# The second pair of feed-forward chunks in seven products, begun on half of the tokens, and three sums of x on GpSimd

## The chip, the cores and the metric

One core of a Trainium2 chip runs the whole kernel. The metric is device time in microseconds (us), the median of several runs. The engines are named as in the profile: PE is TensorE's matmul, PEld its weight load, DVE is VectorE, ACT ScalarE, POOL GpSimd, SP SyncE, which here only starts transfers.

## The reference

A decoder trunk of two layers over 512 tokens of width 1024, in float32. Each layer is a feed-forward (FFN), a mixer (attention and retention) and a second FFN, each followed by a layer norm of the scaled input plus the branch:

```python
def swiglu_ffn(x, w_gu, w_down):
    a, u = jnp.split(x @ w_gu, 2, axis=-1)
    return (jax.nn.silu(a) * u) @ w_down
...
    for l in range(DEPTH):
        x = layer_norm(DEEPNORM_ALPHA * x + 0.5 * swiglu_ffn(x, ffn1_w_gu[l], ffn1_w_down[l]), ln1_g[l], ln1_b[l])
        x = layer_norm(DEEPNORM_ALPHA * x + hybrid_mixer(x, w_in[l], w_out[l], ...), ln2_g[l], ln2_b[l])
        x = layer_norm(DEEPNORM_ALPHA * x + 0.5 * swiglu_ffn(x, ffn2_w_gu[l], ffn2_w_down[l]), ln3_g[l], ln3_b[l])
```

The hidden width of an FFN is 2816: 22 chunks of 128, taken as 11 pairs. There are four FFNs, called A, B, C and D here in the order of time. A begins the program, B follows the first mixer, C follows B directly, and D follows the second mixer.

## The kernel before

**Three matmuls for one.** Every operand is split into a high part (`uh`, `xh`, rounded to the fast matmul type by ACT) and the rest (`ul`, `xl`, a subtraction on DVE); `split` (L173, L174) does both. `mm3` (L188 to L190) multiplies high by high, high by low and low by high into one PSUM bank (`ps`).

**Units.** A weight unit is a split block of 1024 x 128. `Weights` emits the splits of the next units in a given order, up to six units held at once, and loads of 1 MB (`raw`, two buffers, on SP's queue) ahead of them; `done` releases units and so lets the next ones be split. A raw buffer is free for the next load when its last split has read it.

**x and the norms.** x is kept transposed, as `xh` and `xl`, in eight blocks of 128 features by 512 tokens. Each norm (`norm`, DVE, with one small power on GpSimd, L521) finishes 128 tokens of `Y`; `y_to_xT` then transposes them on PE (L488), 8 transposes for 128 tokens, and splits them in two pieces of four blocks each. The transposes run after a number of `step`s of the matmul loops (a task that is `spawn`ed with a delay) or where `finish` forces them out; `pend` holds the four tasks of one norm.

**The gate and up phase (`ffn`).** Before, the first pair of chunks (`fp == 0`) is plain: `glu` makes a and u of one chunk for half of the tokens, 48 matmuls of 256 columns, then silu on ACT and a multiplication on DVE (`gate`, L630 and L631). The second pair (`fp == 1`) is plain too: chunk 2 in halves of the tokens, its a already between the parts of the first pair (`more`), chunk 3 over all 512 columns. From the third pair on (`SEVEN`), `glu7` takes seven block products where the plain form takes eight: x and the weights are cut in 2 x 2 blocks, and sums of blocks are multiplied. A pair then is 14 products of 12 matmuls of 256 columns. Before the first of these pairs, `lead` (L460) issues four matmuls whose result is overwritten.

**Sums of x.** `sums_of_x` makes the sums once per FFN: four additions `xh + xl` (L556), 1024 columns each, into unused chunks of the hidden tile `hT`, then four differences (L560), each split into `Th`, `Tl`. All are on DVE but the high parts. `B[0][0]` and `B[1][0]` are of the first half of the tokens, `B[0][1]` and `B[1][1]` of the second.

**Sums of the weights.** `seven_items` lists a pair's seven units: the first a and u units (`first`), the sums of a (`s12`, `s34`), the last blocks of both (`last`), the sums of u. One `s12` or `s34` pair makes four DVE operations of 512 columns into `S` (L321, L322, L325, L326).

**Order.** A scheduler orders each engine's instructions by the program's order, taking a later one where an earlier is not ready by its own times; each engine then runs its list strictly in order. `mm3`, and until `pin` is cleared the splits too, are held behind what was traced before them on their engine.

Of the kernel before, what the change touches and what calls it, by code (L numbers as in the profile page):

```python
# [15 lines left out]
SEQ = 512  # L16
D = 1024
DFF = 2816
P = 128
# [14 lines left out]
SEVEN = (2, 3, 4, 5, 6, 7, 8, 9, 10)  # L34
# [65 lines left out]
class Trunk:  # L100
# [247 lines left out]
    def ffn_items(self, gu, down, key):  # L348
        items = []
        for fp in range(NFP):  # L350
            a = self.cols_item(gu, fp * 256, (key, "a", fp))
            u = self.cols_item(gu, DFF + fp * 256, (key, "u", fp))
            if fp == 0:
                items += [a[0], u[0], a[1], u[1]]
            else:
                items += self.seven_items(a, u) if fp in SEVEN else a + u
# [179 lines left out]
    def ffn(self, g_, b, out=None):  # L536
        nc, tc, W = self.nc, self.tc, self.W
        with ExitStack() as ctx:
# [8 lines left out]

            def sums_of_x():

                x = hT[:, NF - KC :, :]  # L550
                B = [[x[:, i * H : (i + 1) * H, j * 256 : (j + 1) * 256] for j in range(2)] for i in range(2)]
                for i in range(2):
                    ks = slice(i * H, (i + 1) * H)
                    for j in range(2):
                        ts = slice(j * 256, (j + 1) * 256)
                        nc.vector.tensor_add(B[i][j], self.xh[:, ks, ts].bitcast(F32), self.xl[:, ks, ts].bitcast(F32))  # L556
                        yield 1
                for i, (dst, p_, q_) in enumerate(((B[0][0], B[0][1], B[0][0]), (B[0][1], B[1][1], B[0][1]),
                                                   (B[1][1], B[1][1], B[0][0]), (B[1][0], B[1][0], B[1][1]))):
                    nc.vector.tensor_sub(dst, p_, q_)  # L560
                    self.split(Th[:, i], Tl[:, i], dst)
                    yield 1
# [15 lines left out]
            def glu7(fp):  # L578
# [4 lines left out]
                for m in range(2):  # L583
# [4 lines left out]
                    if fp == SEVEN[0] and m == 0:  # L588
                        self.lead(A[m], u)
# [5 lines left out]
                    nc.vector.tensor_add(Q[m][:, 0], Q[m][:, 0], B[m][:, :256])  # L595
                us = W.get()
                u22 = W.get()
                for m in range(2):
                    C.append(self.ps())
                    u = W.get() if m else us  # L600
                    product(A[m], u, 1, T2, False)
                    nc.scalar.copy(Q[m][:, 1], A[m][:, :256])
                    product(C[m], u, 0, T1)
                    nc.scalar.copy(Q[m][:, 2], C[m][:, :256])
                    W.done()
                    self.step()
# [21 lines left out]
            def gate(f, a, u, t0, t1):  # L628
                sa = gp.tile([P, 768], F32, tag="Q", name=self.nm("Q"), bufs=4)
                nc.scalar.activation(sa[:, : t1 - t0], a[:, : t1 - t0], AF.Silu)  # L630
                nc.vector.scalar_tensor_tensor(out=hT[:, f, t0:t1], in0=u[:, : t1 - t0], scalar=0.5,  # L631
                                               in1=sa[:, : t1 - t0], op0=ALU.mult, op1=ALU.mult)

            def glu(au, f, t0, t1):
                a, u = self.ps(), self.ps()
                self.projs(a[:, : t1 - t0], au[0], t0, t1)
                self.projs(u[:, : t1 - t0], au[1], t0, t1)
                gate(f, a, u, t0, t1)

            for fp in range(NFP):  # L640
                if fp == 0:
                    us = [W.get() for _ in range(6)]
                    self.pin = False
                    au = [us[0:2], us[2:4]]
                    self.finish(self.pend[:2])
                    more = []
                    for t0 in (0, 256):
                        for c in range(2):
                            glu(au[c], c, t0, t0 + 256)
                            if t0:  # L650
                                W.done(2)
                        self.finish(self.pend[2:])
                        if not t0:
                            xs = self.spawn(sums_of_x(), 1)
                        self.pend = []
                        more.append(self.ps())
                        self.projs(more[-1][:, :256], us[4], t0, t0 + 256)
                    W.done()
                    continue
                if fp == 1:  # L660
                    a1, u0 = us[5], W.get()
                    for i in range(2):
                        t0 = i * 256
                        u = self.ps()
                        self.projs(u[:, :256], u0, t0, t0 + 256)
                        gate(2, more[i], u, t0, t0 + 256)
                    W.done()
                    u1 = W.get()
                    glu((a1, u1), 3, 0, SEQ)
                    W.done(2)  # L670
                    continue
# [4 lines left out]
                if fp in SEVEN:  # L676
                    self.finish([xs])
                    glu7(fp)
                    continue
                a0, a1, u0 = W.get(), W.get(), W.get()  # L680
                glu((a0, u0), fp * 2, 0, SEQ)
                W.done(2)
                u1 = W.get()
                glu((a1, u1), fp * 2 + 1, 0, SEQ)
# [518 lines left out]
```

## Time and profile before

| what | value |
|---|---|
| runs | 1752.14, 1753.64, 1753.94 us; median 1753.64 |
| the profiled execution | 1752.16 us, its span 1750.4 us |
| granted clock of TensorE | 0.999 |
| busy: PE, PEld, DVE, ACT, POOL | 99%, 90%, 81%, 53%, 10% of the span |
| DMA | 216.34 MB, mean 124 GB/s |

Times in the rows are counted from the span's start. A row of the timeline gives start, duration, engine, line, operation, result and operands, shape and count, and in brackets the idle time before it with what ended it. A row of groups gives the count, then busy us, mean ns of one, and idle time before with its releaser. A row of windows gives the stretch, then busy time and count of PE, PEld, DVE, ACT and POOL, the clock, and the share and GB/s of DMA. A row of waits gives who waited for whom, us in total, times, and the longest.

### The profile page before, as it was taken

What the parts mean: (1) busy time and instruction counts of PE and PEld (TensorE: products, weight loads), DVE (VectorE), ACT (ScalarE), POOL (GpSimd) and SP (SyncE); (2) the same over time, 40 slices, a digit from 0 to 9 for tenths busy, and PEclk for the clock granted to TensorE, in tenths of its full rate; (3) what the DMA queues carried; (4) which work ended last, traced back from release to release, by engine and by line L of the source; (5) the groups of instructions that cost most, each with busy time, mean ns of one, the idle gap of its engine ahead of it and who ended that gap; (6) DMA issues with size and microseconds to landing.
All of it is one profiled execution on the core that took longest, in us unless ns stands there. A gap on an engine that the chain in (4) does not pass through costs nothing.

```text
span 1750.4 us, 29200 instructions
## 1 busy us (share of the span) xinstructions
PE 1739.2 (99%) x11946; PEld 1580.1 (90%) x11946; DVE 1415.5 (81%) x1975; ACT 927.6 (53%) x1456; POOL 182.7 (10%) x154
## 2 busy tenths in 40 slices
PE   9999999999999999999999999999999999999998
PEld 9999988887789999998899999889877899999886
DVE  7888888856757889879898988988567587988887
ACT  5455656378712455555435556554785234555551
POOL 0000032111111000014000000312011110000231
PEclk9999999999999999999999999999999999999999
DMA  6234389323222243279423334982233123334891
GB/s 193 97 108 134 126 214 220 98 86 95 73 74 73 74 141 101 97 219 217 130 67 109 115 97 157 219 190 91 92 89 97 49 91 103 98 98 144 209 212 48
DMA packets 163765, 216.34 MB, mean 124 GB/s; under 512 B 5168, under 2 KB 116528, under 8 KB 163632
## 3 DMA queue, kind: packets, MB, share of 16 engines
q1 hardware_dynamic: 141872, 172.55, 30.5%
q0 software_dynamic: 21760, 41.95, 13.2%
q8 instruction: 93, 1.52, 0.4%
q14 instruction: 40, 0.33, 0.1%
HBM read 212.38 MB, written 2.10 MB: 123 GB/s over the span
## 4 chain that ended last, share of the span: by engine, by line
PE 48%; DVE 2%; DMA 0%; issue 0%; ACT 0%; POOLq 0%; DVEq 0%; ACTq 0%
PE ps L188 15%; PE ps L189 15%; PE ps L190 15%; PE ps L488 0%; DMA raw<-in_ffn_w_gu_dram 0%; PE ps L1030 0%; PE ps L995 0%; PE ps L1082 0%; PE ps L1022 0%; DVE Y L522 0%; PE ps L1044 0%; DVE ul L174 0%; DVE st L515 0%; DVE Y L513 0%; DVE xl L174 0%; DVE Y L525 0%
## 5 line engine op out<-in xcount | busy, mean ns | idle before, releaser
L188 PE MATMUL ps<-xh,uh 128*128 128x256 f32 (+1 forms) x1616 | 476.0, 295 | 0.0
L189 PE MATMUL ps<-xl,uh 128*128 128x256 f32 (+1 forms) x1616 | 473.0, 293 | 0.5 <-DVE xl L174 0.4
L190 PE MATMUL ps<-xh,ul 128*128 128x256 f32 (+1 forms) x1616 | 473.1, 293 | 0.4 <-DVE ul L174 0.4
L173 ACT CAST uh<-raw 128x1024 fp32r<-128x1024 f32 (+1 forms) x274 | 236.6, 884 | 233.3 <-PE ps L189 127.7
L174 DVE TENSOR_TENSOR ul<-raw,uh 128x1024 fp32r<-128x1024 f32 (+1 forms) x274 | 273.6, 1014 | 56.8 <-ACT uh L173 56.4
L188 PE MATMUL ps<-Th,uh 128*128 128x256 f32 x1152 | 318.0, 276 | 0.0
L189 PE MATMUL ps<-Tl,uh 128*128 128x256 f32 x1152 | 318.0, 276 | 0.0
L190 PE MATMUL ps<-Th,ul 128*128 128x256 f32 x1152 | 318.0, 276 | 0.0
L188 PEld LDWEIGHTS ps<-xh,uh 128*128 128x128 f32 x1616 | 304.1, 188 | 10.5 <-issue 1.6
L190 PEld LDWEIGHTS ps<-xh,ul 128*128 128x128 f32 x1616 | 303.5, 188 | 10.3 <-DVE ul L174 0.8
L189 PEld LDWEIGHTS ps<-xl,uh 128*128 128x128 f32 x1616 | 304.3, 188 | 9.1 <-DVE xl L174 0.9
L188 PE MATMUL ps<-uh,xh 128*128 128x512 f32 x720 | 285.2, 396 | 0.5 <-ACT xh L173 0.5
L189 PE MATMUL ps<-ul,xh 128*128 128x512 f32 x720 | 282.6, 392 | 0.0
L190 PE MATMUL ps<-uh,xl 128*128 128x512 f32 x720 | 281.0, 390 | 0.0
L173 ACT CAST uh<-S 128x1024 fp32r<-128x1024 f32 x144 | 151.3, 1051 | 144.0 <-PE ps L189 140.3
L189 PEld LDWEIGHTS ps<-Tl,uh 128*128 128x128 f32 x1152 | 216.3, 188 | 0.0
L188 PEld LDWEIGHTS ps<-Th,uh 128*128 128x128 f32 x1152 | 216.2, 188 | 0.0
L190 PEld LDWEIGHTS ps<-Th,ul 128*128 128x128 f32 x1152 | 216.2, 188 | 0.0
L174 DVE TENSOR_TENSOR ul<-S,uh 128x1024 fp32r<-128x1024 f32 x144 | 176.0, 1222 | 48.9 <-ACT uh L173 48.4
L394 POOL DMA_DIRECT2D R<-in_ffn_w_down_dram x80 | 97.1, 1217 | 999.8 <-DVE ul L174 912.3
L174 DVE TENSOR_TENSOR ul<-R,uh 128x1024 fp32r<-128x1024 f32 x120 | 145.5, 1223 | 31.5 <-ACT uh L173 31.2
L173 ACT CAST uh<-R 128x1024 fp32r<-128x1024 f32 x120 | 124.8, 1047 | 75.1 <-DMA R<-in_ffn_w_down_dram 36.4
(147 smaller groups left out, 2379.9 us busy)
## 6 DMA issues: line engine op xcount, KB each, us to landing
raw<-in_ffn_w_gu_dram SPq DMA_DIRECT2D x86, 1024.0 KB, 5.3
R<-in_ffn_w_down_dram POOLq DMA_DIRECT2D x80, 512.0 KB, 7.9
raw<-in_w_in_dram SPq DMA_DIRECT2D x18, 1024.0 KB, 5.2
R<-in_ffn_w_down_dram SPq DMA_DIRECT2D x16, 1024.0 KB, 6.2
raw<-in_ffn_w_down_dram SPq DMA_DIRECT2D x12, 1024.0 KB, 7.2
R<-in_ffn_w_down_dram SPq DMA_DIRECT2D x8, 512.0 KB, 4.2
raw<-in_w_in_dram SPq DMA_DIRECT2D x8, 512.0 KB, 5.9
raw<-in_w_out_dram SPq DMA_DIRECT2D x8, 512.0 KB, 6.1
```

The costliest lines, as they stand in the source:

```text
L173: a = self.nc.scalar.copy(hi, src)
L174: b = self.low = self.nc.vector.tensor_sub(lo, src, hi.bitcast(F32))
L188: keep(mm(out, ah, bh, start=start, stop=False, **kw))
L189: keep(mm(out, ah, bl, start=False, stop=False, **kw))
L190: keep(mm(out, al, bh, start=False, stop=stop, **kw))
L394: self.nc.gpsimd.dma_start(src, rows(i, j, g * 2, 2), accum_op=ALU.add))
```

## The change

The second pair joins `SEVEN`. Its first four products (two units, two blocks each) use only the first half of the tokens, so `glu7` is cut by a `yield`: this part runs after the first pair's work on the first half, the rest after the first pair's work on the second half. The transposes of the second half are forced out (`finish`) between the two, after the products begun ahead. `lead` stays at the third pair. In the second part of `glu7`, the product C with `T1` now comes before A with `T2`.

Three of the four additions `xh + xl` go to GpSimd: both of the first half at the start of the FFN, and `B[0][1]` when the second half is there. The differences are reordered, so that `Th[0]` and `Th[2]` come first; one is kept in a `spare` place. The sums run from the point at which the second half is there until the first pair ends. `gate` takes its silu into a tile of 256 columns of the tag `s21`. The first pair's branch for other plain pairs is removed.

```diff
-SEVEN = (2, 3, 4, 5, 6, 7, 8, 9, 10)
+SEVEN = (1, 2, 3, 4, 5, 6, 7, 8, 9, 10)
...
-            if fp == 0:
-                items += [a[0], u[0], a[1], u[1]]
-            else:
-                items += self.seven_items(a, u) if fp in SEVEN else a + u
+            items += self.seven_items(a, u) if fp in SEVEN else [a[0], u[0], a[1], u[1]]
...
+            x = hT[:, NF - KC :, :]
+            B = [[x[:, i * H : (i + 1) * H, j * 256 : (j + 1) * 256] for j in range(2)] for i in range(2)]
+            spare = hT[:, NF - KC - H : NF - KC, :256]
+
+            def whole(eng, i, j):
+                ks, ts = slice(i * H, (i + 1) * H), slice(j * 256, (j + 1) * 256)
+                eng.tensor_add(B[i][j], self.xh[:, ks, ts].bitcast(F32), self.xl[:, ks, ts].bitcast(F32))
+
             def sums_of_x():
...
+                whole(nc.gpsimd, 0, 1)
+                whole(nc.vector, 1, 1)
+                nc.vector.tensor_sub(B[0][0], B[0][1], B[0][0])
+                self.split(Th[:, 0], Tl[:, 0], B[0][0])
+                nc.vector.tensor_sub(spare, B[1][1], B[0][0])
+                self.split(Th[:, 2], Tl[:, 2], spare)
+                yield 1
+                nc.vector.tensor_sub(B[0][1], B[1][1], B[0][1])
+                self.split(Th[:, 1], Tl[:, 1], B[0][1])
+                yield 2
+                nc.vector.tensor_sub(B[1][0], B[1][0], spare)
+                self.split(Th[:, 3], Tl[:, 3], B[1][0])
+                yield 1
...
-                    if fp == SEVEN[0] and m == 0:
+                    if fp == SEVEN[1] and m == 0:
                         self.lead(A[m], u)
...
+                yield
                 us = W.get()
                 u22 = W.get()
                 for m in range(2):
                     C.append(self.ps())
                     u = W.get() if m else us
+                    product(C[m], u, 0, T1)
+                    nc.scalar.copy(Q[m][:, 2], C[m][:, :256])
                     product(A[m], u, 1, T2, False)
                     nc.scalar.copy(Q[m][:, 1], A[m][:, :256])
-                    product(C[m], u, 0, T1)
-                    nc.scalar.copy(Q[m][:, 2], C[m][:, :256])
...
+            us = [W.get() for _ in range(4)]
+            self.pin = False
+            au = [us[0:2], us[2:4]]
+            self.finish(self.pend[:2])
+            for i in range(2):
+                whole(nc.gpsimd, i, 0)
+            for c in range(2):
+                glu(au[c], c, 0, 256)
+            ahead = glu7(1)
+            next(ahead)
+            self.finish(self.pend[2:])
+            self.pend = []
+            xs = self.spawn(sums_of_x(), 0)
+            self.run(xs)
+            for c in range(2):
+                glu(au[c], c, 256, SEQ)
+                W.done(2)
+            self.finish([xs])
+            for _ in ahead:
+                pass
+            for fp in range(2, NFP):
...
+                for _ in glu7(fp):
+                    pass
```

More of the change, by code (lines that the diff above doesn't have):

```diff
@@ L546, in ffn @@
             Tl = gp.tile([P, 4, H, 256], F32R, name=self.nm("Tl"))
-            def sums_of_x():
[L550 to L562, printed above, removed]
+            x = hT[:, NF - KC :, :]
[4 more added lines that the diff above has]
+                eng.tensor_add(B[i][j], self.xh[:, ks, ts].bitcast(F32), self.xl[:, ks, ts].bitcast(F32))
+            def sums_of_x():
+                whole(nc.gpsimd, 0, 1)
[11 more added lines that the diff above has]
+                yield 1
             def product(out, u, ui, b, new=True):
@@ L628, in gate @@
             def gate(f, a, u, t0, t1):
[L629 to L632, printed above, removed]
+                sa = gp.tile([P, 256], F32, tag="s21", name=self.nm("s21"), bufs=2)
+                nc.scalar.activation(sa, a[:, :256], AF.Silu)
@@ L634, in glu @@
+                nc.vector.scalar_tensor_tensor(out=hT[:, f, t0:t1], in0=u[:, :256], scalar=0.5,
+                                               in1=sa, op0=ALU.mult, op1=ALU.mult)
             def glu(au, f, t0, t1):
                 a, u = self.ps(), self.ps()
-                self.projs(a[:, : t1 - t0], au[0], t0, t1)
-                self.projs(u[:, : t1 - t0], au[1], t0, t1)
+                self.projs(a[:, :256], au[0], t0, t1)
+                self.projs(u[:, :256], au[1], t0, t1)
                 gate(f, a, u, t0, t1)
[L640 to L671, printed above, removed]
@@ L675, in ffn @@
                     self.split(*(v.rearrange("p g f t -> p (g f) t") for v in hv), hT[:, HALF : HALF + 4, :256])
[L676 to L684, printed above, removed]
-                W.done(2)
+                for _ in glu7(fp):
+                    pass
             gctx.close()
```

## The prediction

> **What bounds the kernel now.** I read the page first: busy times, clock and the chain.
>
> ```profile
> span 1750.4 us, 29200 instructions
> PE 1739.2 (99%) x11946; PEld 1580.1 (90%) x11946; DVE 1415.5 (81%) x1975; ACT 927.6 (53%) x1456; POOL 182.7 (10%) x154
> ...
> PE 48%; DVE 2%; DMA 0%; issue 0%; ACT 0%; POOLq 0%; DVEq 0%; ACTq 0%
> ...
> raw<-in_ffn_w_gu_dram SPq DMA_DIRECT2D x86, 1024.0 KB, 5.3
> ```
>
> TensorE (PE) is the bound (its clock is 1.00 in the windows below). The view of waits of PE says how little it stands still for others:
>
> ```profile
> PE ps L188 <- ACT xh L173: 0.5, 2, 0.2
> PE ps L189 <- DVE xl L174: 0.4, 1, 0.4
> PE ps L190 <- DVE ul L174: 0.4, 2, 0.2
> ```
>
> The three waits that lie in the layers make 1.3 us in all. So time is the number of matmuls by their spacing, plus whatever new waits an edit makes. Busy time misleads (pipelined matmuls overlap), so I take spacing from starts in the timeline of PE. First the second FFN (B), after the first mixer, with the count from the groups of 561.9 to 584.4 us:
>
> ```profile
> 561.81 0.36 PE L188 MATMUL ps<-xh,uh 128*128 128x256 f32 x1
> 584.51 0.40 PE L188 MATMUL ps<-xh,uh 128*128 128x512 f32 x1
> 595.71 0.28 PE L460 MATMUL ps<-uh 128*128 128x256 f32 x1
> L188 PE MATMUL ps<-xh,uh 128*128 128x256 f32 x64 | 18.1, 282 | 0.0
> ```
>
> From 561.81 to 584.51 stand 3 x 64 = 192 matmuls of 256 columns: 118.2 ns each. Then 48 of 512 columns to 595.71: 233 ns. (The row at 595.71 is the first of the four `lead` matmuls.) VectorE (DVE) is the engine next to the bound, so its windows come next: 46 us at B's start, and 19 us (one pair) of steady seven-product work:
>
> ```profile
> 542.00:588.00 46.00, 46.00 (x355) 44.16 (x354) 45.37 (x59) 18.97 (x27) 2.98 (x2) 1.00 0.28 92
> 640.00:659.00 19.00, 19.00 (x171) 19.00 (x169) 16.84 (x26) 10.58 (x17) 0.00 (x0) 1.00 0.36 113
> ```
>
> DVE (third number) is full for the 46 us in which the sums of x are made, and has 2.2 us to spare in each later pair. The change touches just that full stretch.
>
> **What PE saves.** The second pair has 4 units; before, chunk 2 in halves is 96 matmuls of 256 columns and chunk 3 is 48 of 512: 96 x 0.1182 + 11.20 = 22.55 us in B. With seven products it is 14 x 12 = 168 of 256: 19.86 us at the slow spacing, which I keep because nothing in B's order before the third pair's `lead` changes what PE meets. B and D (the fourth FFN, also behind a mixer): -2.7 each. For the first FFN (A) and the third (C, behind an FFN):
>
> ```profile
> 20.10 0.27 PE L488 MATMUL ps<-ident,Y 128*128 128x128 f32 x1
> 55.61 0.28 PE L460 MATMUL ps<-uh 128*128 128x256 f32 x1
> 887.71 0.27 PE L488 MATMUL ps<-ident,Y 128*128 128x128 f32 x1
> 889.37 0.36 PE L188 MATMUL ps<-xh,uh 128*128 128x256 f32 x1
> 892.69 0.39 PE L189 MATMUL ps<-xl,uh 128*128 128x256 f32 x1
> 911.74 0.39 PE L188 MATMUL ps<-xh,uh 128*128 128x512 f32 x1
> 922.93 0.28 PE L460 MATMUL ps<-uh 128*128 128x256 f32 x1
> ```
>
> C runs faster behind its short hold for x at 892.69: 167 matmuls to 911.74, 114.1 ns each (A has the wait for xl of the view above, and I take the same there). Before, C takes 35.22 us from the transposes to the lead and A 35.51. After, without waits: 48 ahead x 0.118, transposes 1.66, then 96 + 120 at 0.114: 31.9. C -3.3, A -3.6. **All four: -12.3 us**, if nothing waits.
>
> **What the new order exposes.** In A and C the transposes of the second half of the tokens are forced out by `finish`, which now stands behind the 48 products begun ahead. Before, 24 matmuls of the first half (`more`) came between transposes and the first use of that x, and still 3.3 us (889.37 to 892.69) passed. Now nothing stands between:
>
> ```profile
> 890.75 2.48 DVE L174 TENSOR_TENSOR xl<-ps,xh 128x512 fp32r<-128x512 f32 x4
> 889.00 2.07 ACT L173 CAST xh<-ps 128x512 fp32r<-128x512 f32 x4
> 914.59 1.28 DVE L174 TENSOR_TENSOR ul<-raw,uh 128x512 fp32r<-128x512 f32 x2
> 911.88 1.14 ACT L173 CAST uh<-raw 128x512 fp32r<-128x512 f32 x2 [0.61 <-PE ps L189]
> ```
>
> PE needs the third of the four xl. The split of `last`, emitted when the second ahead unit comes free, is ahead in both queues (1.1 us ACT, 1.2 DVE). In C: transposes 893.4 to 895.0; `last` on ACT to 894.5, xh at 0.51 each, the third to 896.1; on DVE `last` to 895.2 and three xl at 0.64 to 897.2: PE stands 2.2 us. Bounds: 0 (transposes put ahead of the products by the scheduler) and 3.3 (as seen before). I take 2.2, twice: **+4.4**.
>
> **GpSimd's three sums.** Its two-input rows and what DVE does beside it:
>
> ```profile
> L974 POOL TENSOR_TENSOR sw<-sw,ropeS 128x256 f32<-128x256 f32 x16 | 11.9, 745 | 46.4 <-ACT sw L972 46.4
> L974 POOL TENSOR_TENSOR sw<-sw,ropeS 128x512 f32<-128x512 f32 x2 | 2.6, 1314 | 9.5 <-ACT sw L972 9.5
> 375.00 1.31 POOL L974 TENSOR_TENSOR sw<-sw,ropeS 128x512 f32<-128x512 f32 x1 [4.77 <-ACT sw L972]
> 375.65 1.21 DVE L174 TENSOR_TENSOR ul<-raw,uh 128x512 fp32r<-128x512 f32 x1
> 1189.15 2.60 POOL L521 TENSOR_TENSOR rs<-mv,mhalf 128x1 f32<-128x1 f32 x1 [3.98 <-DVE mv L519]
> 1190.11 1.22 DVE L174 TENSOR_TENSOR ul<-raw,uh 128x1024 fp32r<-128x1024 f32 x1
> ```
>
> 745 to 1314 ns for 256 more columns: 1024 columns cost about 2.45 us (DVE: 1.22). They do not run beside DVE: the ul at 375.65, normally 0.64 (1.28 for two, above), takes 1.21 and ends 0.55 after GpSimd's; at 1189.15 a one-column GpSimd operation lasts until 0.4 us after DVE's second two-input row. So an add that frees 1.13 us of DVE can hold DVE's two-input work for 2.45. The Trainium skill (SBUF — State Buffer, "SBUF: two separate sides") says that a Vector instruction with two SBUF inputs and a GpSimd one that reads SBUF exclude each other for a whole instruction; the trace agrees in these rows. By that rule, all three adds lost to DVE (7.3 us a start), B and D would each wait 3.4 instead of the 1.4 below, and the time would be 1753.1; with free sharing they would wait 0, A 0.3 less, and it would be 1746.0.
>
> A: the first add is ready with the first xl, and free DVE time is at 8.5:
>
> ```profile
> 8.40 1.28 DVE L174 TENSOR_TENSOR xl<-ps,xh 128x512 fp32r<-128x512 f32 x2
> 9.60 2.04 DVE L174 TENSOR_TENSOR ul<-raw,uh 128x512 fp32r<-128x512 f32 x3
> 10.34 0.39 PE L190 MATMUL ps<-xh,ul 128*128 128x256 f32 x1 [0.15 <-DVE ul L174]
> 19.74 2.00 ACT L173 CAST uh<-raw 128x1024 fp32r<-128x1024 f32 x2 [1.89 <-DMA raw<-in_ffn_w_gu_dram]
> ```
>
> GpSimd holds DVE to 10.95, the ul of 9.60 starts then, and PE, already waiting for it at 10.34, waits 1.3 more. The 96 matmuls then end at 21.4; the ahead unit's ul, behind a load landing at 19.7, ends at 22.0 to 22.3: 0.7 more. **+2.0** (0.0 if the add starts later, 3.0 if the second add also delays a load).
>
> B and D: the whole DVE ledger, spacing from
>
> ```profile
> 552.41 1.22 DVE L174 TENSOR_TENSOR ul<-raw,uh 128x1024 fp32r<-128x1024 f32 x1
> 558.91 1.28 DVE L525 SCALAR_TENSOR_TENSOR Y<-Y,rs,ln 128x1024 f32<-128x1024 f32 x1
> 578.16 1.22 DVE L560 TENSOR_TENSOR hT<-hT 128x1024 f32<-128x1024 f32 x1
> 579.29 1.22 DVE L174 TENSOR_TENSOR Tl<-hT,Th 128x1024 fp32r<-128x1024 f32 x1
> ```
>
> 1.13 start to start for 1024 columns, and 0.64 (half of 1.28) for 512. Two adds now stand among the norms: the last Y (558.91) loses 2.3 us (one add and one weight split) of work ahead and gains about 3.2 of blocking, so the last transposes, and the matmul of 561.81 behind them, come some 0.2 late. The ul of 552.41 goes some 2.3 later, and with it SP's load of the second pair's u columns: issue 556, landing 5.3 later, split by 563.6, needed at 564.9: hidden. The third add's last piece of x is split, as in C, 2.2 after those transposes: it runs from 564.2 to 566.6. After it DVE owes, before PE's last new weights: 9 operations on x 10.2, two sets of weight sums (4 x 0.64 + 1.13) 7.4, `last` 1.3, two splits 2.3, two gates and two adds to Q (256 columns, half of 0.64 each) 1.3: 22.5, so 589.1. PE wants them at 562.0 + (48 + 96 + 72) x 0.118 + 0.2 = 587.7. PE stands 1.4. Bounds 0 and 3.4 (all of 7.3 blocked against 5.3 charged). **+2.8** for both. In C the weights land early and PE is 2.2 later: the same count (15.8 us from 899.5) ends 1.1 before it is needed; cost 0, cover 1.1.
>
> C's product before A's swaps two groups of 12, so that Th[0], made first, is used first; `spare` and the smaller silu tile add no operation: 0. The second pair's additional work for ACT (7 weight splits for 4, and copies) goes into an engine with 8 us free in each steady pair (10.58 of 19); its bytes are the same. Behind the second pair DVE has less lead, but 2.2 us to spare in each of nine pairs. Down phase and mixers keep their code.
>
> **Sum.** -12.3 + 4.4 + 2.0 + 2.8 = -3.1, against the profiled execution's 1752.16 us (1.8 beyond its span, which stays): 1749.1. The median of the three runs, 1753.64, is 1.5 higher; I stay with 1749.1.
>
> **Rivals.** (1) Nearly the full gain: the scheduler places the transposes of A and C ahead of the 48 products (they carry no order against what stands before them), 4.4 vanishes and DVE is in time in B and D: -10.3 to -12.3, 1740 to 1742. For it: x is ready long before in A. Against: in both, PE's earlier products were ready, so order stayed as written. (2) Slower: GpSimd's adds both wait behind DVE's runs, as at 1189.15 (one operation of 1.22), and then block it, 3.6 each, 10.8 a start. DVE would be 3.5 to 5.5 later than charged in four starts; the first 1.1 of it is covered in A and C. From 2.6 more per start the time passes 1757.1; at 3.5: -3.1 + 14 - 2.2 = +8.7, 1760.9. For it: 45.37 of 46 us full. Against: DVE's operations on PSUM leave the way open, and sevens behind have 2.2 spare each. (3) The saving is real but eaten: x exposed for 3.3 twice, as long as C's 889.37 to 892.69: -12.3 + 6.6 + 2.0 + 2.8 = -0.9, 1751.3.
>
> **How the numbers follow.** 0.2% is 3.5 us, about what a measurement here tells from no change, so faster ends at 1750.1 and slower begins at 1757.1. Forecast 0.50 (own range 1745 to 1752: faster 0.31, same 0.19); rival 1 0.20, all faster; rival 2 0.16, slower; rival 3 0.14, same. Faster 0.51, same 0.33, slower 0.16. The range, 1740 to 1757, leaves out the ends of rivals 1 and 2.
>
> **What would show it.** The lead of the third pair in B at about 594.5 instead of 595.71; PE waiting for xl once in A and C, about 2 us; in A the third ul near 10.95 and PE's wait at 10.3 grown to 1.4; GpSimd adds of 2.4 us with DVE rows stretched beside them. The prediction is wrong if transposes stand ahead of the 48 products, if DVE's two-input rows keep 1.22 beside the adds, or if PE waits over 3 us in B.

## The result, and the profile after

| | before | after |
|---|---|---|
| median, us (four runs each) | 1753.63 | 1781.74 |
| runs, us | 1752.14 to 1753.94 | 1777.1, 1777.52, 1785.96, 2029.14 |
| profiled execution, us | 1752.16 | 1777.1 |

The ratio is 1.0153, 95% interval 1.0117 to 1.0189: slower, where 1749.1 was forecast. The run of 2029.14 us was at a clock of 0.80 and is left out of the ratio, though it stands in the median; that of 1785.96 us has no trace, and why it is 8.4 us above the next is not shown. The traces compared are those of the profiled executions, 24.9 us apart. The page of after, span and busy times:

```profile
span 1775.3 us, 29503 instructions
PE 1747.8 (98%) x12042; PEld 1594.2 (90%) x12042; DVE 1461.4 (82%) x2035; ACT 947.5 (53%) x1492; POOL 213.9 (12%) x166
```

Nothing here shows the loss. The start of `lead`, and of the first matmul behind the last seven-product pair, in each FFN does (us from the span's start, from the timelines of PE):

| FFN | `lead`, before | lead, after | end of pairs, before | end of pairs, after | lead to end, before | after |
|---|---|---|---|---|---|---|
| A | 55.61 | 61.04 | 227.47 | 239.59 | 171.86 | 178.55 |
| B | 595.71 | 610.34 | 767.57 | 788.89 | 171.86 | 178.55 |
| C | 922.93 | 944.95 | 1094.79 | 1116.81 | 171.86 | 171.86 |
| D | 1463.06 | 1487.91 | 1634.92 | 1659.76 | 171.86 | 171.85 |

Two things went wrong. **The stretches that end at the lead** grew, each counted from the end of the pairs before: A by 5.4 us, B 2.5 (368.24 to 370.75), C 0.7, D 2.8; 11.5 in all. **The nine later pairs, which the change does not touch**, took 6.7 us more in A and in B: 13.4. (The growth of A is known to some 2 us only: in before_mid_lead below, whose code is that of before up to there, the same `lead` starts at 57.28 us, 1.7 later. B, C and D differ by at most 0.7, 0.4 and 0.1 us among the traces of kernels that are that of before up to the lead.) The first part has its rows in the waits of PE, the second has none there, since nobody waits. It is found in counts of matmuls in equal windows (before, then after; the second number in brackets is PE's count):

```profile
100.00:200.00 100.00, 100.00 (x885) 100.00 (x884) 89.19 (x133) 55.96 (x85) 0.00 (x0) 1.00 0.33 106
640.00:740.00 100.00, 100.00 (x885) 100.00 (x884) 89.19 (x134) 56.07 (x85) 0.00 (x0) 1.00 0.33 106
```

```profile
100.00:200.00 100.00, 100.00 (x851) 100.00 (x850) 85.29 (x126) 53.26 (x81) 0.00 (x0) 1.00 0.34 110
640.00:740.00 100.00, 100.00 (x851) 100.00 (x850) 85.62 (x128) 53.91 (x83) 0.00 (x0) 1.00 0.33 106
970.00:1070.00 100.00, 100.00 (x884) 100.00 (x884) 89.09 (x134) 56.14 (x85) 0.00 (x0) 1.00 0.33 106
1500.00:1600.00 100.00, 100.00 (x885) 100.00 (x884) 89.44 (x135) 55.76 (x85) 0.00 (x0) 1.00 0.33 107
```

PE is 100% busy at clock 1.00 in all six rows, and yet does 885 or 851 matmuls in 100 us: 113 or 117.5 ns each. Matmuls of 256 columns have two steady spacings here, called fast (113 ns) and slow (118 ns) from here on. After's timeline of PE shows where they change: A, then C.

```profile
60.36 0.28 PE L188 MATMUL ps<-Th,uh 128*128 128x256 f32 x1
61.04 0.63 PE L457 MATMUL ps<-uh 128*128 128x256 f32 x4
61.51 0.28 PE L188 MATMUL ps<-xh,uh 128*128 128x256 f32 x1
61.98 0.28 PE L189 MATMUL ps<-xl,uh 128*128 128x256 f32 x1
...
944.25 0.28 PE L188 MATMUL ps<-Th,uh 128*128 128x256 f32 x1
944.95 0.64 PE L457 MATMUL ps<-uh 128*128 128x256 f32 x4
945.79 0.28 PE L188 MATMUL ps<-xh,uh 128*128 128x256 f32 x1
946.35 0.28 PE L190 MATMUL ps<-xh,ul 128*128 128x256 f32 x1
```

In A the six matmuls from 60.36 to the lead go at 113 ns, and the four from 61.51 to 61.98 at 118. In C it is 117 before the lead and 112 behind it. `lead` turned one spacing into the other, in both directions.

The waits of PE, 1.3 us within the layers before:

```profile
PE ps L188 <- ACT Q L610: 4.7, 4, 2.0
PE ps L190 <- DVE ul L174: 4.4, 7, 1.1
PE ps L188 <- DVE Q L616: 4.3, 4, 2.0
PE ps L188 <- ACT xh L173: 2.2, 4, 0.9
PE ps L189 <- DVE xl L174: 1.6, 2, 0.9
```

Half of this (L610, L616) is a wait that the prediction never had: for the read-outs of banks that go on accumulating in the second pair. (A read-out here is the copy, or the addition, of a bank's partial result into `Q`.) B, from the timelines of GpSimd, DVE, ACT and PE:

```profile
556.98 5.75 POOL L551 TENSOR_TENSOR hT<-xh,xl 128x1024 f32<-128x1024 f32 x2 [8.73 <-DVE xl L174]
558.31 2.16 DVE L174 TENSOR_TENSOR ul<-raw,uh 128x1024 fp32r<-128x1024 f32 x1
560.46 3.36 DVE L519 SCALAR_TENSOR_TENSOR Y<-Y,mv,ln 128x1024 f32<-128x1024 f32 x1
...
578.44 2.40 POOL L551 TENSOR_TENSOR hT<-xh,xl 128x1024 f32<-128x1024 f32 x1 [6.87 <-DVE xl L174]
578.88 2.51 DVE L321 TENSOR_TENSOR S<-raw 128x512 f32<-128x512 f32 x1
...
595.64 1.05 ACT L173 CAST uh<-S 128x1024 fp32r<-128x1024 f32 x1 [2.31 <-DVE S L326]
...
599.29 0.39 PE L188 MATMUL ps<-Th,uh 128*128 128x256 f32 x1 [2.04 <-ACT Q L610]
...
608.85 0.39 PE L188 MATMUL ps<-Th,uh 128*128 128x256 f32 x1 [1.96 <-DVE Q L616]
```

Beside GpSimd's adds these three DVE rows, which take 1.22, 1.28 and 0.68 us elsewhere, take 2.16, 3.36 and 2.51: 4.85 us more. DVE is late; ACT stands idle 2.31 us for DVE's `S` at 595.64, with the copy of a bank queued behind that cast; PE cannot go on accumulating in that bank before it is copied. The Trainium skill (SBUF — State Buffer, "SBUF: two separate sides") says that a GpSimd instruction that reads SBUF and a DVE one with two SBUF inputs exclude each other for a whole instruction; these rows agree.

In A and C stands most of the rest of the list: `ul` behind GpSimd's first two adds, and x of the second half.

```profile
8.51 5.55 POOL L551 TENSOR_TENSOR hT<-xh,xl 128x1024 f32<-128x1024 f32 x2 [7.11 <-DVE xl L174]
...
11.88 0.39 PE L190 MATMUL ps<-xh,ul 128*128 128x256 f32 x1 [1.12 <-DVE ul L174]
14.67 0.39 PE L190 MATMUL ps<-xh,ul 128*128 128x256 f32 x1 [1.14 <-DVE ul L174]
...
917.45 0.38 PE L188 MATMUL ps<-xh,uh 128*128 128x256 f32 x1 [0.87 <-ACT xh L173]
918.59 0.38 PE L189 MATMUL ps<-xl,uh 128*128 128x256 f32 x1 [0.77 <-DVE xl L174]
```

In D a wait of 2 us at 1476.81 is followed by a spell at half clock (the last number but two is the clock), 15 matmuls started in 3.19 us at 213 ns, some 1.4 us lost:

```profile
1478.06:1481.25 3.19, 3.19 (x18) 3.19 (x16) 2.97 (x4) 1.59 (x3) 0.00 (x0) 0.50 0.00 0
```

The Trainium skill (TensorE: Matmul & The Clock Gate, "Part 1: The HAM clock gate") gives two clock states, full and half, decided in windows of about 3.4 us; the 0.50 agrees, and so does the length, since the clock is at half from 1478.06 to 1481.47 in this trace, 3.41 us. In that part of the Trainium skill the half clock follows an idle window; PE waited 2.05 us here, and what brought the spell is not shown.

### The profile page after: what moved, and what is told of

Read it like the earlier page. It is cut to its first block, busy times and chain, and to the rows that moved or that the text cites. A ratio compares the mean times of both kernels' runs of the same rounds, so it can differ in the third digit from the quotient of the medians.

```text
span 1775.3 us, 29503 instructions
## 1 busy us (share of the span) xinstructions
PE 1747.8 (98%) x12042; PEld 1594.2 (90%) x12042; DVE 1461.4 (82%) x2035; ACT 947.5 (53%) x1492; POOL 213.9 (12%) x166
## 4 chain that ended last, share of the span: by engine, by line
PE 90%; DVE 7%; DMA 1%; issue 1%; ACT 0%; POOLq 0%; DVEq 0%; SPq 0%; ACTq 0%
PE ps L188 28%; PE ps L189 28%; PE ps L190 28%; DVE ul L174 2%; DMA raw<-in_ffn_w_gu_dram 1%; PE ps L485 1%; PE ps L1017 1%; PE ps L982 1%; PE ps L1069 1%; PE ps L1009 1%; PE ps L1031 1%; DVE Tl L174 1%; DVE xl L174 1%; DVE Y L519 0%; PE ps L1065 0%
## 5 line engine op out<-in xcount | busy, mean ns | idle before, releaser
L188 PE MATMUL ps<-xh,uh 128*128 128x256 f32 (+1 forms) x1520 | 445.0, 293 | 1.9 <-ACT xh L173 1.7
L190 PE MATMUL ps<-xh,ul 128*128 128x256 f32 (+1 forms) x1520 | 442.2, 291 | 3.5 <-DVE ul L174 3.5
L189 PE MATMUL ps<-xl,uh 128*128 128x256 f32 (+1 forms) x1520 | 441.9, 291 | 1.6 <-DVE xl L174 1.6
L188 PE MATMUL ps<-Th,uh 128*128 128x256 f32 x1280 | 357.9, 280 | 9.1 <-ACT Q L610 4.7
L190 PE MATMUL ps<-Th,ul 128*128 128x256 f32 x1280 | 357.1, 279 | 0.8 <-DVE ul L174 0.8
L189 PE MATMUL ps<-Tl,uh 128*128 128x256 f32 x1280 | 357.0, 279 | 0.0
L188 PEld LDWEIGHTS ps<-Th,uh 128*128 128x128 f32 x1280 | 240.6, 188 | 10.9 <-ACT Q L610 5.8
L190 PEld LDWEIGHTS ps<-Th,ul 128*128 128x128 f32 x1280 | 243.1, 190 | 1.2 <-DVE ul L174 1.2
L189 PEld LDWEIGHTS ps<-Tl,uh 128*128 128x128 f32 x1280 | 240.5, 188 | 0.0
L174 DVE TENSOR_TENSOR ul<-S,uh 128x1024 fp32r<-128x1024 f32 x160 | 194.8, 1221 | 40.4 <-ACT uh L173 40.4
```

The source lines that it names most:

```text
L174: b = self.low = self.nc.vector.tensor_sub(lo, src, hi.bitcast(F32))
L188: keep(mm(out, ah, bh, start=start, stop=False, **kw))
L189: keep(mm(out, ah, bl, start=False, stop=False, **kw))
L190: keep(mm(out, al, bh, start=False, stop=stop, **kw))
```

## The experiments

### What sets the spacing: without lead, and with 512-column matmuls ahead of it

**before_no_lead**, later timed again as **before_no_lead_5**; **after_no_lead** is the same edit in the changed kernel.

```diff
-                    if fp == SEVEN[0] and m == 0:
-                        self.lead(A[m], u)
```

> The kernel before without the four lead matmuls. Theory P (two paces: the 512-column matmuls leave the stream at the slow pace of 118 ns per 256 columns, and the four lead matmuls turn it into the fast one of 113): all four FFNs run their nine seven-product pairs at 118, 1515 matmuls x 4.4 ns = 6.7 us each, so about 1752 + 4 x 6.7 - 4 x 0.5 = 1777 us. Rival L (the lead only fills a wait, and the slow pace of the changed kernel's first two FFNs comes from its heavier DVE or from GpSimd): the pace stays 113, and the time falls by 4 x 0.5 to about 1750.

> The changed kernel without the four lead matmuls. Theory P: the lead turns the pace whichever it is, so the first two FFNs (fast just before the lead, slow behind it) now stay fast, and the last two (slow before, fast behind) now stay slow; the time stays near 1777 - 2 = 1775 us, with the 13.4 us moved from the first two FFNs to the last two. Rival L: the first two stay slow (118) and the last two fast (113), and the time is 1775 as well; the paces by FFN tell the two apart, not the time.

**after_set_lead**: the changed kernel, in `lead`:

```diff
+        for _ in range(4):
+            ... self.nc.tensor.matmul(out, u[0][:, 0, :], u[0].rearrange("p k c -> p (k c)")[:, :512], ...)
         for _ in range(4):
             ... matmul(out[:, :256], u[0][:, 0, :], u[0].rearrange("p k c -> p (k c)")[:, :256], ...)
```

> The changed kernel with four matmuls of 512 columns in front of the four lead matmuls. Theory P: 512-column matmuls bring the slow pace whatever was before, and the lead then turns it into the fast one, in all four FFNs: 1777 - 2 x 6.7 + 4 x 0.93 = 1767.4 us. Rival L: the first two FFNs stay at 118, and the time is 1777 + 3.7 = 1780.8.

before_no_lead gave 1750.74 us (before beside it: 1755.01), with all four FFNs at 113 ns: behind its 48 products of 512 columns the kernel before was fast without lead, in that run, so its number is rival L's. after_no_lead gave 1777.50, with A and C slow, B and D fast, which neither side had expected; each FFN went on at the spacing that it had just ahead of the third pair (118 ns in A and C, 113 to 114 in B and D). after_set_lead gave 1767.64, all four fast, where theory P had 1767.4. I took this for "512-column matmuls make the spacing fast"; act_wholes_only below shows that this was wrong.

> The kernel before without its lead, timed in five rounds. One run gave 1750.74 against 1755.01. The 16 matmuls left out are worth 16 x 0.118 = 1.9 us, and the trace of that run shows the fast spacing in all four FFNs without them: ratio 0.998 to 0.999, so faster than both kernels by 1.5 to 4 us against before. Rival (the spacing behind the 512-column matmuls is drawn anew in each execution, and lead made it safe): some executions 6.7 us longer, ratio 1.000 or above.

Twelve runs: nine from 1750.0 to 1753.5, three from 1758.2 to 1760.2; ratio 1.0003 (0.9992 to 1.0015). So it is not faster. The step between the groups is about that of one slow FFN (6.7 us; the three runs have no trace), and before, with lead, had no such run among the 17 beside it (1751.9 to 1755.0).

### A lead in the middle of a running stream

**before_mid_lead**: nothing waits, nothing else is changed.

```diff
-                    if fp == SEVEN[0] and m == 0:
+                    if fp in (SEVEN[0], SEVEN[4]) and m == 0:
                         self.lead(A[m], u)
```

> The kernel before with the four lead matmuls also put ahead of the seventh pair (fp 6), in the middle of a stream of 256-column matmuls that runs at 113.3 ns. Nothing is made to wait by this. Theory (the spacing has two values, and a disturbance of the running stream draws it anew): behind the new lead the five last pairs, about 840 matmuls, go on at 117.8 ns in most of the four FFNs, 3.8 us each; with 4 x 0.45 us for the additional matmuls, 1765 to 1772 against about 1755 for before on this chip. Rival (only waits for other engines change the spacing): 113.3 ns to the end, 1756.8.

1771.06 us, before beside it 1752.55. Windows of 60 us before and behind the new lead in A:

```profile
70.00:130.00 60.00, 60.00 (x532) 60.00 (x531) 53.19 (x80) 33.36 (x52) 0.00 (x0) 1.00 0.33 106
140.00:200.00 60.00, 60.00 (x511) 60.00 (x511) 50.90 (x76) 32.28 (x49) 0.00 (x0) 1.00 0.33 106
```

532 matmuls, then 511; the windows of B, C and D say the same. Four matmuls change the spacing of the next 800, four times of four.

**before_mid_plain**: at that place the four stream `xh[:, 0, :256]`, not the weight tile itself.

> As before_mid_lead, but the four matmuls ahead of the seventh pair stream x (xh, as the product behind them does) and not the weight tile itself. Theory A (any four matmuls that break the order of three in the stream draw the spacing anew): slow behind them in most FFNs, 1767 to 1772 as in before_mid_lead (1771.1). Theory B (it is what lead reads, its own stationary tile as the moving one, that shifts the stream): no change of spacing, 4 x 0.45 us more than before, about 1754.5.

1754.77 (before 1753.0): theory B. The row of the same window as above:

```profile
140.00:200.00 60.00, 60.00 (x532) 60.00 (x531) 53.05 (x79) 33.59 (x52) 0.00 (x0) 1.00 0.33 106
```

So it is not any disturbance: in these four places matmuls whose moving operand is their own weight tile shifted the stream, and matmuls that stream x did not.

### The stretches up to the lead: GpSimd, the place of finish, VectorE

**after_sums_dve**: the three sums on DVE. **set_sums_dve**: the same on after_set_lead.

```diff
-                whole(nc.gpsimd, 0, 1)
+                whole(nc.vector, 0, 1)
...
-                whole(nc.gpsimd, i, 0)
+                whole(nc.vector, i, 0)
```

> The changed kernel with the three sums of x on VectorE instead of GpSimd. Theory G (GpSimd's adds hold up VectorE's two-input operations for 2.4 us each): PE's two waits of 1.3 us for the first units' low parts in the first FFN go, the last wait of the norms in the second and fourth FFN shrinks, VectorE has 3 x 1.13 us more to do but loses 4.9 us of blocking: up to the lead each FFN gets shorter, about 2.5 us in the first and 1 to 1.5 in the second and fourth. Rival D (VectorE is simply too full): with 3.4 us more of its own work each FFN's stretch up to the lead gets longer by 1 to 3 us. The pace behind the lead may come out either way in each FFN (6.7 us each), so the stretches are compared, not the totals.

> The kernel after with the four 512-column matmuls ahead of lead, and the three sums of x on VectorE instead of GpSimd. Theory (GpSimd's adds hold VectorE longer than the adds would take there, 4.85 us against 3 x 1.13 in B): the waits for ul at 11.74 and 14.54 us in A (2.3 us together) go, B and D wait 1 to 2 us less each, C is unchanged: 1762 to 1764. Rival (GpSimd does take work off a full VectorE): A gains 2.3, B and D lose 3.4 less what was blocked, total 1767 to 1770.

after_sums_dve gave 1788.76, with all four FFNs slow (26.8 us of pace), which is why the next kernels have the 512-column matmuls. set_sums_dve gave 1761.12, 6.5 below after_set_lead, and the waits at 11.74 and 14.54 us in A are gone. These are single runs, and the runs of before beside them differ by 2.5 us themselves (1755.01, 1752.55), so it is better to compare the stretches up to the first matmul of lead, from the profiled executions. The table has what each is longer than in before, in us:

| run | A | B | C | D |
|---|---|---|---|---|
| after | +5.4 | +2.5 | +0.7 | +2.8 |
| after_sums_dve | +7.3 | +1.4 | 0.0 | +0.6 |
| after_set_lead | +5.7 | +2.5 | +0.9 | +2.7 |
| set_sums_dve | +2.3 | +1.6 | -0.1 | +0.8 |
| set_finish_first | +4.5 | +2.5 | +0.9 | +2.4 |
| set_no_tl | +5.3 | +0.4 | +0.5 | +0.2 |
| set_dve_finish | +2.9 | +1.0 | -1.5 | +0.7 |
| set_dve_finish_no_tl | -0.7 | -2.8 | -2.4 | -2.7 |
| act_wholes | +0.1 | -1.7 | -2.4 | -1.8 |
| before_gp_sums | +2.5 | +1.4 | +0.3 | +1.4 |

With the sums on DVE, B, C and D are 0.7 to 2.3 us shorter in both pairs of kernels (spells at half clock, one to three in each of the four traces, are part of this): GpSimd's adds cost more than they relieve. before_gp_sums below, which has no such spell, says the same. In A the two differ. set_sums_dve gains 3.3 us; after_sums_dve loses 1.8, but its trace has a wait of 2.35 us for the weights `uh` at 22.43 us and 10.2 us at half clock there, so A of that run says nothing of the edit.

**before_gp_sums**: the converse, three of the four sums of before on GpSimd.

```diff
-                        nc.vector.tensor_add(B[i][j], ...)
+                        eng = nc.vector if i and j else nc.gpsimd
+                        eng.tensor_add(B[i][j], ...)
```

> The kernel before with three of its four sums of x on GpSimd, and nothing else of the change. Theory (each such add holds VectorE for 2.4 us where its own add took 1.13 us, and VectorE is full at the start of B and D): B and D 2 to 4 us longer up to the lead, A and C 0 to 2, spacing fast behind it since 512-column matmuls stand ahead of the lead: 1757 to 1763 against 1752 to 1755 for before. Rival (GpSimd takes work off VectorE at no price): within 1.5 us of before, or below it.

1757.87 (before 1753.0): +4.9, spacing fast, within the expected total. B and D grew by 1.4 us each, less than the 2 to 4 expected; A by 2.5, with the waits for `ul` that A of after has (here 1.17 and 1.14 us, at 11.20 and 13.98). PE's waits for DVE, which were 0.4 us for `ul`, 0.4 for `xl` and none for `Y` in before:

```profile
PE ps L190 <- DVE ul L174: 2.5, 3, 1.2
PE ps L189 <- DVE xl L174: 2.2, 3, 1.0
PE ps L488 <- DVE Y L525: 1.4, 2, 0.7
```

PE waits for DVE's work, not for GpSimd's own results: the sums there lose by what they block.

**set_finish_first**: on after_set_lead.

```diff
             ahead = glu7(1)
-            next(ahead)
             self.finish(self.pend[2:])
+            next(ahead)
```

> The kernel after, with four 512-column matmuls ahead of lead (spacing fast in all FFNs, 1767.6 in its one run), and finish(pend[2:]) moved ahead of the 48 products of the second pair. Theory (x of the second half is exposed by the place of finish): the waits for xh and xl behind the transposes in A and C, 1.7 and 1.8 us, vanish, nothing moves in B and D where the transposes were already done: 1764.1. Rival (the wait only moves to another operand, since VectorE makes the same splits in the same time): within 1 us of 1767.6.

1766.21, 1.4 less: nearer the rival. By the table nearly all of it lies in A, which differs by more than that between executions (after_set_lead has a wait of 0.9 us for the weights `uh` there), and C, whose exposure of x the edit was to end, is as long as without it. So no gain is shown. The waits for x went (`xl` from 1.8 us to none, `xh` from 2.2 to 0.5), and those on Q grew, from 4.4 and 3.7 (L614 and L620 here are L610 and L616 of after):

```profile
PE ps L188 <- ACT Q L614: 7.1, 4, 2.0
PE ps L188 <- DVE Q L620: 5.6, 4, 2.6
```

**set_no_tl**: on after_set_lead.

```diff
-                self.split(Th[:, i], Tl[:, i], ...)
+                nc.scalar.copy(Th[:, i], ...)
...
-                return Th[:, i], Tl[:, i]
+                return Th[:, i], Th[:, i]
```

> The kernel after with the four 512-column matmuls ahead of lead, and without the low parts of the four sums of x: VectorE makes no Tl (four operations of 1024 columns fewer for each FFN), and the products use Th in its place, so TensorE has the same matmuls. Theory (VectorE's full stretch sets the late read-outs and splits, so the waits in B and D are its lateness): 4 x 1.13 = 4.5 us less work there takes away the waits on Q and ul ahead of the lead in B (3.2 us) and D (4.5 us with its spell) and the last one in A (0.95): about 1760 against 1767.6. Rival (the order on ScalarE, where the read-out copy stands behind a cast that waits for S, sets them by itself): the waits for the copies stay, no less than 1766.

This kernel leaves the low parts of the sums out of the result. 1762.2, 5.4 less: most of the 7.6 expected, and 4.6 of it in B and D. PE's waits for the copies fell from 4.4 to 2.7 us and for DVE's additions from 3.7 to 2.2.

**set_dve_finish** joins the lead with 512 columns, DVE's sums and the early finish; **set_dve_finish_no_tl** leaves Tl out of it as well.

> The three repairs of the changed kernel together: four 512-column matmuls ahead of lead, sums of x on VectorE, finish(pend[2:]) ahead of the 48 products. From set_sums_dve (1761.1) less the 1.4 us that the earlier finish was worth beside it: 1759 to 1760.5, still above before. If VectorE is what ends all that remains, the earlier finish is worth nothing more and it stays at 1761.

> set_dve_finish (1761.5 us; TensorE waits 9.8 us for VectorE's additions to Q, 3.3 each in B and D, 0.8 in C and 3.1 in A) without the low parts of the sums of x, as in set_no_tl: 4 x 1.13 = 4.5 us less for VectorE at each start, the same matmuls. Theory (a full VectorE is all that is left of the loss, and the saving on TensorE is real behind it): the waits on Q go to under 2 us in all, and with the half-clock spells behind them the time falls to 1749 to 1753, about that of before, although each stretch still holds 0.9 us of 512-column matmuls. Rival (the read-outs of the accumulated banks wait for something else, ScalarE's order or the banks themselves): waits of 2 us stay at each start, 1757 or more.

1761.46 and 1747.22 (before beside them: 1753.0 and 1751.22). The first is what was expected if the earlier finish is worth nothing more. The first line is of set_dve_finish; in the second kernel PE has no wait for `Q` at all, and the longest that is left in the layers is for `ul`:

```profile
PE ps L188 <- DVE Q L620: 9.8, 7, 2.0
```

```profile
PE ps L190 <- DVE ul L174: 1.1, 3, 0.8
```

That is 14.2 us (12.5 against the runs of before beside them) for 4.5 us of DVE's work at each of four starts. What was left of the loss was DVE's full ledger, and the saving on PE lies behind it: by the table, B and D are 2.8 and 2.7 us shorter than before. The 1747.2 still holds 16 matmuls of 512 columns (0.93 us in each FFN), so an estimate without them is some 7.7 us below before, for a kernel that leaves the low parts out.

### A version that computes everything

**act_wholes**: set_dve_finish, with x of the second half copied by ACT from the transposes' bank, where DVE added `xh + xl`.

```diff
         self.split(xh[:, c0 : c0 + 4, ts], xl[:, c0 : c0 + 4, ts], bv)
+        if dst is None and self.wholes is not None:
+            nc.scalar.copy(self.wholes[c0 // 4][t // 2][:, :, t % 2 * P : t % 2 * P + P], bv)
```

> set_dve_finish with the two sums xh + xl of the second half of the tokens replaced by copies that ScalarE makes of x itself, from the bank that the transposes filled. It computes the whole result. VectorE has 2 x 1.13 = 2.3 us less at each start, half of what set_dve_finish_no_tl took away; ScalarE has eight copies of 128x512, about 0.5 us each, more. Theory (VectorE's full ledger): the waits on Q (9.8 us) fall by 2.3 in B, D and A and go in C, the half-clock spells partly with them: 1751 to 1756, no worse than before by more than 0.2%. Rival (ScalarE's queue, now with more ahead of the read-out copies, takes over): 1758 or more.

Median 1751.4 of ten (1750.05 to 1758.55; before 1753.05); ratio 0.9997 (0.9987 to 1.0006). The waits for DVE's additions fell from 9.8 to 2.9 us: half of the relief took away 10 of the 14 us.

What it spends on spacing, 1.39 us in each FFN, was varied next: **act_wholes_two** has two 512-column matmuls ahead of lead, **act_wholes_only** four and no lead behind them.

> act_wholes with two 512-column matmuls, not four, ahead of the four of lead. Two fewer in each FFN are 8 x 0.231 = 1.8 us. Theory (any such matmul or two leads the stream into the fast spacing): 1749.5, ratio 0.998, with slow draws (a further 6.7 us) in no more than 1 run of 10. Rival (it takes four): slow draws in a third of the runs or more, ratio 1.000 or above.

> act_wholes with the four 512-column matmuls and without the four of lead behind them. 16 x 0.117 = 1.9 us less: 1749.5, ratio 0.998, if the 512-column matmuls alone set the spacing. If the lead behind them is what keeps it, as the three runs of twelve at 1758 to 1760 of the kernel before without its lead suggest, a quarter of the runs lie some 7 us higher and the ratio is 0.999 to 1.001.

act_wholes_two: 1757.64 (twelve runs, 1754.66 to 1768.62), ratio 1.0033 (1.002 to 1.0046). act_wholes_only: 1776.35 (four runs, 1775.55 to 1776.57), ratio 1.0129 (1.0114 to 1.0143). Both expectations failed. In the profiled execution of act_wholes_two C came at 118 ns to its six matmuls (two of 512 columns, four of lead) and went on so; A, B and D came at 113 to 114 and went on fast. So these six left the spacing as it was, in all four places: C stayed slow, and the further groups of runs would be what the waits drew. In the second kernel all four FFNs are slow behind the matmuls of 512 columns, A, B and D too, which came fast. The windows are of C in act_wholes_two and of A in act_wholes_only:

```profile
980.00:1080.00 100.00, 100.00 (x851) 100.00 (x850) 85.02 (x126) 53.16 (x82) 0.00 (x0) 1.00 0.34 110
```

```profile
100.00:200.00 100.00, 100.00 (x851) 100.00 (x851) 85.55 (x128) 53.29 (x81) 0.00 (x0) 1.00 0.34 111
```

So four 512-column matmuls of this kind leave the stream slow, and it is lead behind them that makes it fast, as it was in all 28 FFNs of the seven profiled kernels with four of each. That is the theory of the toggle, and the last two runs use it. **act_wholes_c** has no 512-column matmuls and lead in C alone; **act_wholes_bare** has nothing there at all.

> act_wholes without the 512-column matmuls, and with the four of lead in the third FFN (C) alone. In the traces of its three versions A, B and D reach the third pair at 113 ns behind their last wait (nine of nine) and C, which does not wait, at 118 (three of three). Theory (lead turns either spacing into the other): all four FFNs go on at 113.3 ns; 4 x 1.39 us of extra matmuls become 0.47: 1751.4 - 5.1 = 1746.3, ratio 0.996 to 0.997, faster than both kernels. Rival (without lead the spacing behind a wait is drawn anew in each execution): one to three FFNs slow in many runs, 1753 to 1766.

> The same without lead in C as well: nothing but the products. Theory (toggle): A, B and D fast, C slow behind its slow start: 1746.3 - 0.47 + 6.7 = 1752.5, so 6.2 us above act_wholes_c. Rival (C falls back to 113 ns by itself, or the spacing is drawn by chance): within 2 us of act_wholes_c, or spread over 1746 to 1766.

act_wholes_c: 1752.56 (before 1753.79), ratio 0.9989 (0.9977 to 1.0001). Eleven runs: three at 1746.3 to 1747.3, seven at 1752.5 to 1753.7, one at 1759.9. act_wholes_bare: 1753.91, ratio 1.0009 (0.9999 to 1.0019), eight runs at 1751.6 to 1754.5, four at 1758.4 to 1759.8. C as expected (first with lead, then without), but D of act_wholes_c, behind a wait, went on slow in the profiled execution:

```profile
980.00:1080.00 100.00, 100.00 (x885) 100.00 (x884) 88.22 (x130) 57.50 (x87) 0.00 (x0) 1.00 0.35 117
1520.00:1620.00 100.00, 100.00 (x851) 100.00 (x851) 85.02 (x128) 54.49 (x82) 0.00 (x0) 1.00 0.34 107
```

```profile
980.00:1080.00 100.00, 100.00 (x852) 100.00 (x851) 85.60 (x127) 53.80 (x82) 0.00 (x0) 1.00 0.34 111
```

Both theories hold in part: lead toggles, and a wait seems to draw the spacing anew in each execution. The groups of runs lie as far apart as one slow FFN; the one run of act_wholes_c that has a trace, with D slow, took 1752.98 us and lies in the middle group. The other runs have none, so this is argued from the times. By it the lowest, 1746.3 to 1747.3, are what the idea is worth with all four fast, some 7 us under before; no version here gets it each time, and none is shown to be faster than before.

## Why the prediction was wrong

By its own steps, against growth of the stretches in the table of leads. Forecast per stretch: A -3.6 + 2.2 + 2.0 = +0.6, measured +5.4; B and D -2.7 + 1.4 = -1.3 each, measured +2.5 and +2.8; C -3.3 + 2.2 = -1.1, measured +0.7. The misses make 14.5 us, the pace of later pairs 13.4, together 27.9 of the 28.0 between 1749.1 and 1777.1. (That is arithmetic on the traces; the growth of A is uncertain by some 2 us, as said.)

**Failed: "which I keep because nothing in B's order before the third pair's lead changes what PE meets".** The sum had no term for the nine later pairs, taking the spacing behind the lead as a given. The prediction's own rows held both spacings (118.2 ns in B, 114.1 in C "behind its short hold") and I used them for stretches of 200 matmuls, not asking what 4.5 ns would be over 1515: 6.8 us. The change removed the 512-column products from the place ahead of lead and put waits there; then A and B reached the lead fast, and were turned slow. after_set_lead, with all four fast, took this part away: 1767.64, which is 1777.1 less 13.4 and, by estimate, plus 3.7 for 16 matmuls of 512 columns. Shown: lead as a toggle of a running stream (before_mid_lead, before_mid_plain, and the rows of A and C above). Not settled: why matmuls that stream their own weight tile do this, why the six of act_wholes_two did not, and what a wait leaves behind.

**Mis-sized: "All four: -12.3 us", for the same reason.** It took C and A behind the hold for x at 114 ns. Where nearly nothing waits (set_dve_finish_no_tl) they run at 118, and the stretches save 2.4 us in C, not 3.3, and 0.7 in A, not 3.6 (with a late start and a wait for `ul` in it); B and D save 2.8 and 2.7, as forecast. Together 8.6 us.

**Failed: the ledger of B and D, "PE stands 1.4".** The two rows of B above are 4.0 us by themselves. The ledger took PE's last new weights as DVE's only deadline. The second pair brings earlier ones: each of the banks that `glu7` calls A and C is read (copy on ACT, addition on DVE) in the middle of its accumulation, and these read-outs stand in order behind casts and sums for later units. Counting instructions was right in kind: 4.5 us less for DVE took away the waits on `Q` (set_dve_finish_no_tl). The bound of 3.4 was set by the wrong deadline.

**Mis-sized: A, +2.0 for GpSimd's first adds.** For the first add 1.3 was forecast, for a later unit 0.7. The rows have 1.12 and 1.14 at two `ul`s (11.88, 14.67), since the second add, back to back with the first, blocked the next unit's `ul`; and the second pair's waits on Q were missed here as in B.

**Right.** The exposure of x in A and C: 2.2 forecast, 2.1 measured in each (in C the two rows above, 0.87 and 0.77 us of waiting, stand 1.15 us each behind the matmul before, not 0.12), and the transposes stayed behind the 48 products. The add on GpSimd: 2.45 forecast, 2.40 in the row; it holds DVE, and three of them cost 4.9 us in before. The condition named for failure, PE waiting over 3 us in B, is what came.

**Near by luck: rival 2 in B and D.** The stretches came out 3.8 and 4.1 us longer than charged, where it had DVE 3.5 us late. But its mechanism, 3.6 us for each add, was not the case: the adds took 2.4 to 2.9 us each and lengthened DVE's rows in B by 4.85 us, less than the 5.3 charged. The rest is the read-outs.

**Mis-sized: rival 1's price.** It took the 4.4 us of exposure as recoverable. set_finish_first ended the waits for x by hand, and the stretch of C was as long as before the edit: the waits on `Q` grew instead.

## What to carry to other kernels

Where an engine is 99% full (DVE, 45.37 of 46 us at the start of B), list every point in the stretch at which another waits for it, read-outs of accumulating banks included, and not the last one only; moving work to a neighbour that locks it out is no relief. Look up the steady spacing of the bound engine's instructions on both sides of an edit, as counts in equal windows: if two spacings occur, price the other one over all that follows. When single runs lie in groups, find the step between them before comparing medians.

## What the runs showed of the hardware

Two spacings of 256-column matmuls at full clock with PE 100% busy, 113 and 118 ns, each kept for over 1500 matmuls. Four matmuls that stream their own weight tile turned fast into slow or slow into fast in each of twelve places where they, and nothing else of the kind, met a running stream of 256 columns at full clock (before_mid_lead 4, after 4, after_sums_dve 3, act_wholes_c 1); four that stream x, in before_mid_plain, left it as it was. Four of 512 columns on their own weight tile left the stream slow in all four FFNs (act_wholes_only), the same and four of 256 behind them left it fast in all 28, and two and four left it as it was in all four (act_wholes_two). Behind a wait the spacing came out either way (fast in A, slow in D of act_wholes_c); that it differs between executions of one kernel is argued from groups of run times that lie some 6 to 7 us apart. And in eight of the profiled kernels the clock stands at half for spells of 3.41 us, as in D above, or twice that (after_sums_dve in A). All eight have waits of 1 to 2 us, but not each such wait brings a spell: act_wholes_c has a wait of 1.96 us in A and no spell behind it.
